# A gradient over rows: stores on a second DMA queue, issued in pairs with loads, the load held back by a pass of DVE

## The chip, the cores and the metric

The kernel runs on one core of one Trainium2 chip. The metric is the device time of one execution in microseconds (us), as a median over runs; lower is better. The profile is of one execution, and its own times count from the first instruction of the program. VectorE is called DVE, GpSimd POOL, ScalarE ACT and SyncE SP, as in the profile.

## The reference

```python
x = np.random.randn(8192, 8192).astype(np.float32)
np.gradient(x, axis=1)
```

For each of 8192 rows of 8192 float32 values: inside the row, element j of the result is half of x[j+1] - x[j-1]; at the two ends it is the one-sided difference, x[1] - x[0] and x[8191] - x[8190], not halved. 268.44 MB are read and 268.44 MB are written.

## The kernel before

The 8192 rows are cut into 32 sets (`nsets`) of 256 rows. A set is two neighbouring rows on each of 128 partitions (`R = 2`), so a partition holds 2 x 8192 = 16384 contiguous float32, 64 KB, and one transfer of a set is 8.39 MB. On chip there are three slots (`NB = 3`), each of 64 + 16384 columns. A load writes set i into columns 64 and up of slot i mod 3 (`SH = 64`); the result is built in the same slot from column 0 on, 64 columns to the left of what it is made from, and is stored from there.

For each set, in the order of the program:

- POOL (L70) computes the four unhalved end differences of each partition (two rows, two ends) into the small tile `ends`. It waits for the load of the set.
- DVE (L76) makes one custom pass over 16382 columns: element j+2 minus element j, times 0.5. It waits for POOL. At the four places that are row ends it writes values of no use.
- DVE or, for twelve of the sets, POOL (L87) copies the four values from `ends` over those places.
- SP (L89) issues the store of the set.

Everything that moves data is issued by SP, so there is one DMA queue, in the order in which SP issues. Three loads are issued at the start. After every third set, three more loads follow, and load i waits for the store of set i - 3, which used the same slot. The queue so carries three stores, then three loads, and so on; the last group has two of each.

`manual_schedule` keeps the order as written. The helper `chain` takes the place of the automatic dependencies: an instruction waits for those that are named as `needed`, and for the one in front of it on its engine where that one belongs to the same slot.

Of the kernel before, what the change touches and what calls it, by code (L numbers as in the profile page):

```python
# [1 line left out]

# [4 lines left out]


@with_exitstack
def kernel(  # L10
    ctx: ExitStack,
    tc: tile.TileContext,
    x: bass.AP,
    out: bass.AP,
):

    nc = tc.nc
    P = nc.NUM_PARTITIONS
    n, m = x.shape
    R = 2
    NB = 3  # L30
    SH = 64
    W = R * m
    nsets = n // (P * R)
    f32 = x.dtype

    x_sets = x.rearrange("(s p t) m -> s p (t m)", p=P, t=R)
    out_sets = out.rearrange("(s p t) m -> s p (t m)", p=P, t=R)

    pool = ctx.enter_context(tc.tile_pool(name="pool", bufs=1))
    slots = [pool.tile([P, SH + W], f32, name=f"slot{k}", tag=f"slot{k}") for k in range(NB)]  # L40
    ends = pool.tile([P, nsets, R, 2], f32, name="ends", tag="ends")
    loads, stores = [], [None] * nsets
    in_front = {}

    def chain(i, ins, *needed):

        group, engine = f"slot{i % NB}", ins.ins.engine
        keep = [o.ins for o in needed]  # L50
        if in_front.get(engine, (None,))[0] == group:
            keep.append(in_front[engine][1])
        tc.declare_no_dep(ins.ins, group=group, keep=keep, reason="implied by the needed step")
        tc.add_to_no_dep_group(group, ins.ins)
        in_front[engine] = group, ins.ins
        return ins

    def load(i):
        b = slots[i % NB]
        ins = nc.sync.dma_start(out=b[:, SH : SH + W], in_=x_sets[i])  # L60
        loads.append(chain(i, ins, *([stores[i - NB]] if i >= NB else [])))

    with tc.manual_schedule():
        for i in range(NB):
            load(i)
        for i in range(nsets):
            b = slots[i % NB]
            xin = b[:, SH : SH + W].rearrange("p (t m) -> p t m", m=m)

            ins = nc.gpsimd.tensor_sub(  # L70
                out=ends[:, i, :, :],
                in0=xin[:, :, 1 : m : m - 2],
                in1=xin[:, :, 0 : m - 1 : m - 2],
            )
            at = [chain(i, ins, loads[i])]
            ins = nc.vector._custom_dve(  # L76
                dve_ops.TENSOR_TENSOR_REDUCE_SUB_MAX,
                out=b[:, 1 : W - 1],
                in0=b[:, SH + 2 : SH + W],
                in1=b[:, SH : SH + W - 2],  # L80
                s0=0.0,
                s1=0.5,
            )
            halved = chain(i, ins, *at)
            res = b[:, 0:W].rearrange("p (t m) -> p t m", m=m)
            placer = nc.gpsimd if i % 5 in (1, 3) and i < nsets - 2 else nc.vector
            ins = placer.tensor_copy(out=res[:, :, 0 : m : m - 1], in_=ends[:, i, :, :])  # L87
            placed = chain(i, ins, halved)
            ins = nc.sync.dma_start(out=out_sets[i], in_=b[:, 0:W])  # L89
            stores[i] = chain(i, ins, placed)  # L90
            if i % NB == NB - 1:
                for k in range(i + 1, min(i + 1 + NB, nsets)):
                    load(k)


# [1 line left out]
_INS = ['x']  # L97
_OUTS = [((8192, 8192), 'float32')]


# [23 lines left out]
```

## Time and profile before

| | |
|---|---|
| time, median of 3 runs | 1248.12 us (1246.43 to 1248.73) |
| span of the profiled execution | 1245.7 us; its own time is not listed beside it |
| DVE busy | 554.6 us (45%), 52 instructions |
| POOL busy | 8.8 us (1%), 48 instructions |
| DMA queue q1 | 9216 packets, 536.88 MB, 99.8% of 16 engines' span |
| DMA rate | 431 GB/s, mean over the span |
| L76, the pass over a set | 32 times, mean 17224 ns |
| L87, the copy of the ends | 20 times on DVE, mean 172 ns; 12 times on POOL, mean 190 ns |
| L70, the end differences | 32 times on POOL, mean 198 ns |
| issue to landing, median | loads 58.0 us, stores 40.4 us |

How to read it: busy times of an engine are the sum of its instructions' durations; issuing a DMA is not counted as busy. A DMA transfer is spread over 16 DMA engines, and each engine works through its own share of rows; a transfer has landed when all 16 have reported. "From issue to landing" therefore includes the time that a transfer stands in the queue behind others. In the timeline a row has the start, the duration, the engine, the line, the operation, and in brackets how long the engine had been idle and what ended that. A row of a table of windows has the window and its length, busy time and number of instructions of DVE and POOL, the clock, and then the DMA engines' share and rate; a packet is counted in the window in which it begins, so in short windows the share can be over 1.

### The profile page before, as it was taken

What the parts mean: (1) busy time and instruction counts of PE and PEld (TensorE: products, weight loads), DVE (VectorE), ACT (ScalarE), POOL (GpSimd) and SP (SyncE); (2) the same over time, 40 slices, a digit from 0 to 9 for tenths busy, and PEclk for the clock granted to TensorE, in tenths of its full rate; (3) what the DMA queues carried; (4) which work ended last, traced back from release to release, by engine and by line L of the source; (5) the groups of instructions that cost most, each with busy time, mean ns of one, the idle gap of its engine ahead of it and who ended that gap; (6) DMA issues with size and microseconds to landing.
All of it is one profiled execution on the core that took longest, in us unless ns stands there. A gap on an engine that the chain in (4) does not pass through costs nothing.

```text
span 1245.7 us, 237 instructions
## 1 busy us (share of the span) xinstructions
DVE 554.6 (45%) x52; POOL 8.8 (1%) x48
## 2 busy tenths in 40 slices
DVE  2850583069009702850582079009603840591083
POOL 0000000000000000000000000000000000000000
DMA  9999999999999999999999999999999999999999
GB/s 404 438 436 423 427 431 438 438 438 436 436 427 431 425 438 436 425 434 436 429 434 436 434 436 434 436 434 438 419 436 436 434 438 438 431 434 429 429 410 404
DMA packets 9217, 536.88 MB, mean 431 GB/s; under 512 B 1024, under 2 KB 1024, under 8 KB 1024
## 3 DMA queue, kind: packets, MB, share of 16 engines
q1 hardware_dynamic: 9216, 536.88, 99.8%
q14 instruction: 1, 0.01, 0.0%
HBM read 268.44 MB, written 268.44 MB: 431 GB/s over the span
## 4 chain that ended last, share of the span: by engine, by line
another core or an unknown queue 74%; DVE 18%; DMA 3%; issue 2%; POOL 1%; SPq 0%; POOLq 0%
DVE slot L76 18%; DMA slot<-in_x_dram 3%; POOL ends L70 0%; POOL slot L87 0%; SPq L60 0%; POOLq L119 0%; DVE slot L87 0%
## 5 line engine op out<-in xcount | busy, mean ns | idle before, releaser
L76 DVE CUSTOM_DVE_ANT_0 slot<-slot 128x16382 f32<-128x16382 f32 x32 | 551.2, 17224 | 668.7 <-POOL ends L70 668.7
L70 POOL TENSOR_TENSOR ends<-slot 128x4 f32<-128x4 f32 x32 | 6.3, 198 | 989.6 <-DMA slot<-in_x_dram 989.6
L87 POOL COPY slot<-ends 128x4 f32<-128x4 f32 x12 | 2.3, 190 | 207.9 <-DVE slot L76 207.9
L87 DVE COPY slot<-ends 128x4 f32<-128x4 f32 x20 | 3.4, 172 | 0.7
L108 POOL MEMSET const-bfloat16-1.0<- 128x1 bf16 x1 | 0.1, 101 | 0.0
L108 POOL MEMSET const-uint8-127<- 128x1 uint8 x1 | 0.1, 101 | 0.0
L108 POOL MEMSET const-float32-0.0<- 128x1 f32 x1 | 0.1, 98 | 0.2 <-issue 0.2
L108 POOL MEMSET const-float32-1.0<- 128x1 f32 x1 | 0.1, 98 | 0.0
## 6 DMA issues: line engine op xcount, KB each, us to landing
slot<-in_x_dram SPq DMA_DIRECT2D x32, 58.0
out_dram<-slot SPq DMA_DIRECT2D x32, 40.4
```

Source lines behind the costliest of these rows:

```text
L70: ins = nc.gpsimd.tensor_sub(out=ends[:, i, :, :], in0=xin[:, :, 1 : m : m - 2], in1=xin[:, :, 0 : m - 1 : m - 2],)
L76: ins = nc.vector._custom_dve(dve_ops.TENSOR_TENSOR_REDUCE_SUB_MAX, out=b[:, 1 : W - 1], in0=b[:, SH + 2 : SH + W], in1=b[:, SH : SH + W - 2],
L87: ins = placer.tensor_copy(out=res[:, :, 0 : m : m - 1], in_=ends[:, i, :, :])
L108: nc = _bacc.Bacc("TRN2", target_bir_lowering=False, num_devices=1)
```

## The change

Stores are issued by ACT, loads by SP, each in a queue of its own. Two loads are issued at the start instead of three. From then on load i + 2 (`ahead`) belongs to store i.

Before the copy of the ends of set i, DVE makes a pass of 8 columns (`FIRST`) that waits for the landing of store i - 1 (for i from 1 to 30); the copy, and with it store i, come after it on DVE. After the copy, DVE makes a pass of 1700 columns (`THEN`), and load i + 2 waits for that pass. Both passes read a tile of zeros, `still`, which POOL sets once, and write into the slot that load i + 2 will overwrite, the one that store i - 1 has left. They are the same custom operation as the pass over a set, and their results are not used. All copies of the ends are made by DVE.

```diff
-    def load(i):
+    def load(i, *needed):
         b = slots[i % NB]
         ins = nc.sync.dma_start(out=b[:, SH : SH + W], in_=x_sets[i])
-        loads.append(chain(i, ins, *([stores[i - NB]] if i >= NB else [])))
+        loads.append(chain(i, ins, *needed))
+
+    def difference(out, x, width):
+        return nc.vector._custom_dve(
+            dve_ops.TENSOR_TENSOR_REDUCE_SUB_MAX,
+            out=out,
+            in0=x[:, 2 : 2 + width],
+            in1=x[:, 0:width],
+            s0=0.0,
+            s1=0.5,
+        )
+
+    def pause(i, at, width, *needed):
+        ins = difference(slots[i % NB][:, at : at + width], still, width)
+        return chain(i, ins, *needed)
 
     with tc.manual_schedule():
-        for i in range(NB):
+        for i in range(NB - 1):
             load(i)
...
             halved = chain(i, ins, *at)
             res = b[:, 0:W].rearrange("p (t m) -> p t m", m=m)
-            placer = nc.gpsimd if i % 5 in (1, 3) and i < nsets - 2 else nc.vector
-            ins = placer.tensor_copy(out=res[:, :, 0 : m : m - 1], in_=ends[:, i, :, :])
+            ahead = i + NB - 1
+            if 0 < i < nsets - 1:
+                pause(ahead, SH, FIRST, stores[i - 1])
+            ins = nc.vector.tensor_copy(out=res[:, :, 0 : m : m - 1], in_=ends[:, i, :, :])
             placed = chain(i, ins, halved)
-            ins = nc.sync.dma_start(out=out_sets[i], in_=b[:, 0:W])
+            ins = nc.scalar.dma_start(out=out_sets[i], in_=b[:, 0:W])
             stores[i] = chain(i, ins, placed)
-            if i % NB == NB - 1:
-                for k in range(i + 1, min(i + 1 + NB, nsets)):
-                    load(k)
+            if ahead < nsets:
+                load(ahead, pause(ahead, SH + FIRST, THEN))
```

`FIRST, THEN = 8, 1700` stands with the other constants, and `still` is `pool.tile([P, 2 + THEN], f32)`, set by `nc.gpsimd.memset(still, 0.0)` ahead of the loops.

More of the change, by code (lines that the diff above doesn't have):

```diff
@@ L31 @@
     SH = 64
+    FIRST, THEN = 8, 1700
     W = R * m
@@ L41 @@
     ends = pool.tile([P, nsets, R, 2], f32, name="ends", tag="ends")
+    still = pool.tile([P, 2 + THEN], f32, name="still", tag="still")
+    nc.gpsimd.memset(still, 0.0)
     loads, stores = [], [None] * nsets
@@ L75 @@
             at = [chain(i, ins, loads[i])]
[L76 to L83, printed above, removed]
+            ins = difference(b[:, 1 : W - 1], b[:, SH : SH + W], W - 2)
             halved = chain(i, ins, *at)
             res = b[:, 0:W].rearrange("p (t m) -> p t m", m=m)
-            placer = nc.gpsimd if i % 5 in (1, 3) and i < nsets - 2 else nc.vector
-            ins = placer.tensor_copy(out=res[:, :, 0 : m : m - 1], in_=ends[:, i, :, :])
+            ahead = i + NB - 1
+            if 0 < i < nsets - 1:
+                pause(ahead, SH, FIRST, stores[i - 1])
+            ins = nc.vector.tensor_copy(out=res[:, :, 0 : m : m - 1], in_=ends[:, i, :, :])
             placed = chain(i, ins, halved)
-            ins = nc.sync.dma_start(out=out_sets[i], in_=b[:, 0:W])
+            ins = nc.scalar.dma_start(out=out_sets[i], in_=b[:, 0:W])
             stores[i] = chain(i, ins, placed)
-            if i % NB == NB - 1:
-                for k in range(i + 1, min(i + 1 + NB, nsets)):
-                    load(k)
+            if ahead < nsets:
+                load(ahead, pause(ahead, SH + FIRST, THEN))
 _INS = ['x']
```

## The prediction

> **What bounds the kernel now.** I read the page first: engines, DMA rows, queues.
>
> ```profile
> DVE 554.6 (45%) x52; POOL 8.8 (1%) x48
> DMA  9999999999999999999999999999999999999999
> GB/s 404 438 436 423 427 431 438 438 438 436 436 427 431 425 438 436 425 434 436 429 434 436 434 436 434 436 434 438 419 436 436 434 438 438 431 434 429 429 410 404
> DMA packets 9217, 536.88 MB, mean 431 GB/s; under 512 B 1024, under 2 KB 1024, under 8 KB 1024
> q1 hardware_dynamic: 9216, 536.88, 99.8%
> ```
>
> The 16 DMA engines are the bound: one queue, busy 99.8% of a span of 1245.7 us, while VectorE (DVE) works 45% of it. 9216 packets are 64 transfers x 16 engines x 9: eight rows of 64 KB and one 4-byte completion. The change moves the same bytes, so it can win only what the queue loses to slow packets, and it can lose whatever makes an engine wait or slows a packet.
>
> To see what is lost I took the timeline. A `POOL L70` starts about 0.07 us after a load has landed, so its start times are the landings:
>
> ```profile
> 22.71 0.20 POOL L70 TENSOR_TENSOR ends<-slot 128x4 f32<-128x4 f32 x1 [22.27 <-DMA slot<-in_x_dram]
> 42.04 0.20 POOL L70 TENSOR_TENSOR ends<-slot 128x4 f32<-128x4 f32 x1 [19.13 <-DMA slot<-in_x_dram]
> ...
> 62.44 0.20 POOL L70 TENSOR_TENSOR ends<-slot 128x4 f32<-128x4 f32 x1 [2.69 <-DMA slot<-in_x_dram]
> ...
> 954.88 0.20 POOL L70 TENSOR_TENSOR ends<-slot 128x4 f32<-128x4 f32 x1 [59.57 <-DMA slot<-in_x_dram]
> ...
> 974.22 0.20 POOL L70 TENSOR_TENSOR ends<-slot 128x4 f32<-128x4 f32 x1 [19.15 <-DMA slot<-in_x_dram]
> ...
> 993.55 0.20 POOL L70 TENSOR_TENSOR ends<-slot 128x4 f32<-128x4 f32 x1 [19.13 <-DMA slot<-in_x_dram]
> ```
>
> Load 1 lands 19.33 us after load 0, load 2 another 20.40 us later; in the late group both steps are 19.33 to 19.34. A load followed by a load takes 19.33 to 19.36 everywhere. The third load of a group, which has a store behind it in the queue, takes 20.40, 19.45, 19.51, 20.05, 19.85, 19.79, 19.45, 19.84, 19.33, 19.36 in the ten groups: mean 19.70, so a change from load to store costs 0.36 us on average, 0 to 1.06, and 3.6 us in all. A change from store to load shows nothing over 0.05. The windows show the same in packets (a row counts the packets that begin in it):
>
> ```profile
> 57.90:60.37 2.47, 1.60 (x1) 0.19 (x1) 1.00 1.42 425
> 60.37:61.42 1.05, 0.00 (x0) 0.00 (x0) 1.00 0.00 0
> 61.42:62.10 0.68, 0.00 (x0) 0.00 (x0) 1.00 3.57 1542
> 1204.62:1205.39 0.77, 0.00 (x0) 0.00 (x0) 1.00 0.00 0
> 1205.46:1205.60 0.14, 0.00 (x0) 0.00 (x0) 1.00 16.42 7022
> ```
>
> The first three: load 2's last packets begin at about 58 and should end 2.42 us later, but no packet begins for another 1.05 us. The last two price a store's start from nothing: store 30 is issued at 1204.62 while 15 engines are idle, no data begins before 1205.39, and the 15 first packets come at 1205.47 to 1205.59, 0.85 to 0.97 us after issue (each 2.45 us instead of 2.42).
>
> **The change, part by part.** Each queue now has one direction. Per iteration DVE waits for store i-1, does an 8-column pass, copies the two end columns, store i leaves from ScalarE's (ACT) queue, DVE passes 1700 columns, load i+2 leaves from SP. So store i and load i+2 share the engines; I call that a pair, and there are 30 (stores 0 to 29 with loads 2 to 31).
>
> Seam, from the landing of store i-1 to the first packet of store i: last packet to semaphore 0.40 us (store 30: last data at 1225.16, last update at 1225.56); semaphore to DVE about 0.07 (as POOL above); the pass of 8 columns about 0.17 (17.22 us for 16382 columns is 1.04 ns a column and some 0.16 fixed); 0.03; the copy 0.17 (L87, mean 172 ns); 0.03 to the issue; 0.85 to 0.97 to data. Sum 1.72 to 1.84 us. ACT issues no DMA in this trace; I price its start like SP's row, bound it by zero and by the coldest row (the first load: issue 0.74, first packets 1.75 to 2.43, so up to 1.7), and take 0.91 because it is the warm one. With 1.7 the seam is 2.55.
>
> Its cover is the tail of load i+1. The pass of 1700 columns takes 1700 x 1.04 ns + 0.16 = 1.93 us, so the load comes about 1.98 us behind its store, inside the store's first packet (2.42). If the engines take packets from the two queues in turn, they do store, load, store, load, and each ends with one load packet of 2.41 us after the last store packet. 2.41 covers 1.72 to 1.84 with about 0.6 to spare; an engine that is ahead of the slowest by more than that idles, but only to be level with it. Nothing is lost at the seam then. If that cover were gone, it is 1.8 us x 30 = 54.
>
> DVE's waiting instruction has the copy, the 1700 pass and the difference of set i+1 behind it. After store i-1 lands at T, the pass ends at about T+2.4, which is when load i+1 lands; the difference ends at T+20, and the next store lands at T+38.7. Per pair DVE has 17.22 + 0.17 + 0.17 + 1.93 = 19.5 us of work: 18 us of slack. The twelve copies that go from POOL (190 ns) to DVE (172) and the memset of 1702 columns (POOL idles 22.27 us first) are under this cover: nothing. SP no longer holds stores between loads; its new wait is for the 1700 pass only, with only later loads behind.
>
> The beginning stays: loads 0 and 1, then store 0, ready at 40.40 and at the engines at 41.3, when load 1's data is ending (landed 41.98). The end stays covered too: store 30 leaves when store 29 has landed, beside load 31's tail; store 31 is ready 17.22 + 0.17 + 0.2 after load 31 lands, inside store 30's 19.34.
>
> The sum: landing of load 0 at 22.71, then 63 transfers x 19.34 = 1218.4, then 0.83 from the last landing to the span's end as now (1244.84 to 1245.67), less the 0.07 counted twice: 1241.9 us against 1245.7. That is 3.8 less: the ten direction changes (3.6) and a little at store 30. The runs' median, 1248.12, stands 2.4 above the profiled span (the lowest run 0.8 above, the profiled run's own time is not given beyond its span), so 1248.1 - 3.8 = 1244.3.
>
> What this leaves open is the price of alternating. No row has two queues at work. The nearest is the direction change within one queue, 0 to 1.06 us. With 8 changes from load to store in each of 30 pairs, 240 in all, zero is lost at the low end and 87 us at the mean price (254 at the highest). I take zero for the forecast: the delay sits in the last load packet of a queue whose next transfer goes the other way, all engines show it even when they reach that point 3 us apart, and in the changed kernel no queue ever turns. That is an inference and not a row, hence the odds below. Below zero there is nothing much: 2.42 us per 64 KB is what every undisturbed packet takes, in either direction.
>
> One rule speaks against taking turns row by row. The Trainium skill, "DMA: Bandwidth & Descriptors", section "Queues, rings and completion order", says that an engine goes round its queues a whole packet at a time, a packet being typically 9 to 17 descriptors; no run here shows which unit that is on these queues. The Trainium skill, same page, section "Anatomy of one DMA" puts a transfer's fixed cost at about 2.0 us where the store's rows here give 0.4 + 0.9; by it the estimated seam would be 2.5 us, not 1.8, and the cover of 2.41 just used up.
>
> **The rivals.**
>
> 1. *Whole transfers alternate.* If an engine drains all nine entries of the store before it looks at the load, the order is store, load, store, load by transfers, the seam has 19 us of cover, but the engine turns once per pair: 30 x 0.36 = 10.9 on 1244.3 gives 1255, slower. For it: the nine entries belong to one transfer. Against: nothing in the trace. It turns the gain into a loss once a turn costs over 3.8 / 30 = 0.13 us. (The packet of 9 to 17 descriptors in the Trainium skill, "DMA: Bandwidth & Descriptors", section "Queues, rings and completion order", would do this here.)
>
> 2. *Every change from load to store costs, across queues too.* 240 x 0.36 = 87 gives 1331; at 0.02, which the two best groups do not exceed, 4.8 gives 1249. Break-even with before is 3.8 / 240 = 16 ns a change, and eight of the ten groups show over 0.1 us. For it: the only row on mixed directions. Against: the two late groups, and the argument above. I see it spread between 1249 and 1331.
>
> 3. *The seam is not covered.* If the load does not outlast the store, because the two share unevenly or the load's first packet comes first on some engines (then the store ends last), each pair idles: 0.3 us x 30 = 9 gives 1253, 1.8 x 30 gives 1298. For it: a margin of only 0.6 us, and engines up to 3 us apart late in the trace. Against: the shared wait brings them level in each pair, and the slowest engine never idles while the 0.6 holds.
>
> 4. *It does nothing that can be measured*: part of the 3.8 is given back. A difference under 0.2% (2.5 us; the three runs spread over 0.18%) cannot be told from none.
>
> **How the numbers follow.** Forecast mechanism 0.46, its own range 1242 to 1248: 0.38 of it is faster by over 0.2% (under 1245.6), 0.08 within. Rival 1: 0.16. Rival 2: 0.22. Rival 3: 0.10. Rival 4: 0.04 within, and 0.02 for an end earlier than I can account for. Faster 0.40, same 0.12, slower 0.48: the likeliest single case is the gain, but the slower cases together outweigh it. The range runs from 1241 to 1300: it takes in rivals 1 and 3 and the lower half of 2, and leaves out the upper part of 2 (0.12) and the earliest ends (0.03).
>
> **What would show it.** Right: the landings of consecutive loads 38.6 to 38.7 us apart from load 2 to load 31; a store's landing about 2.4 us before its partner load's; issue of the next store about 0.9 us after that landing; DMA share of the two queues near 100% in sum; slow load packets gone. Rival 1: store to landing about 20 us instead of 37, landings of loads 19 us after the stores'. Rival 2: a pair over 39 us with no engine idle and packets above 2.42 us. Rival 3: the pair long, packets at 2.42 us, and windows without packet starts after each store's landing. If DVE's difference ends later than the store it should precede, the slack of 18 us was wrong.

## The result, and the profile after

The changed kernel takes 1300.22 us (median, 1297.22 to 1302.07) against 1248.07 us: ratio 1.0416, 95% interval 1.0401 to 1.0431. It is 4.2% slower; forecast were 1244.3 us and a range up to 1300.0.

The page after, the lines that answer to those of before:

```profile
DVE 613.8 (47%) x124; POOL 8.1 (1%) x37
DMA  9999999999999999999999999999999999999998
GB/s 419 387 419 419 419 419 419 419 419 419 419 415 391 419 418 419 387 389 419 450 389 411 395 419 419 419 415 403 407 419 419 419 419 413 425 405 401 419 419 387
DMA packets 9217, 536.88 MB, mean 413 GB/s; under 512 B 1024, under 2 KB 1024, under 8 KB 1024
q10 hardware_dynamic: 4608, 268.44, 49.7%
q1 hardware_dynamic: 4608, 268.44, 49.6%
```

The same 9216 packets and bytes, now half on each queue. The engines are "busy" for 49.7 + 49.6 = 99.3% of a span of 1300.3 us, hardly less than the 99.8% of before. So most of the lost time did not go into gaps but into longer packets: 0.993 x 1300.3 x 16 / 8192 = 2.52 us per 64 KB row, where before has 0.998 x 1245.7 x 16 / 8192 = 2.43.

Where the long rows are, the timeline says. One seam of the changed kernel:

```profile
241.53 0.17 DVE L56 CUSTOM_DVE_ANT_0 slot<-still 128x8 f32<-128x8 f32 x1 [19.70 <-DMA out_dram<-slot]
241.62 0.16 DVE L88 COPY slot<-ends 128x4 f32<-128x4 f32 x1
241.69 1.92 DVE L56 CUSTOM_DVE_ANT_0 slot<-still 128x1700 f32<-128x1700 f32 x1
241.81 0.34 ACTq L90 DMA_DIRECT2D out_dram<-slot  x1
243.64 0.33 SPq L52 DMA_DIRECT2D slot<-in_x_dram  x1
243.98 0.20 POOL L76 TENSOR_TENSOR ends<-slot 128x4 f32<-128x4 f32 x1 [39.40 <-DMA slot<-in_x_dram]
```

A store has landed just before 241.53; 0.28 us later the next store is issued (241.81), 1.83 us after that its load (243.64), and the old load lands 2.45 us after the old store (243.98). All of this is as forecast. The pair is not: from landing to landing of the loads (`POOL L76` starts) it takes 39.45 to 42.06 us, from 83.97 to 1260.17 on average 40.56, instead of 38.6 to 38.7. The windows of this seam and of another show what is late (a row is counted where it begins; 1 MB in a window is 16 rows, one per engine):

```profile
243.00:243.50 0.50, 0.50 (x1) 0.00 (x0) 1.00 6.64 2097
243.50:246.10 2.60, 2.00 (x2) 0.20 (x1) 1.00 0.00 0
246.10:247.00 0.90, 0.90 (x1) 0.00 (x0) 1.00 2.69 1165
488.25:488.35 0.10, 0.10 (x1) 0.00 (x0) 1.00 1.78 655
525.70:526.60 0.90, 0.00 (x0) 0.00 (x0) 1.00 0.01 0
526.70:528.08 1.38, 1.08 (x3) 0.00 (x0) 1.00 0.00 0
528.10:528.30 0.20, 0.20 (x1) 0.00 (x0) 1.00 11.56 4915
528.30:530.50 2.20, 1.61 (x2) 0.20 (x1) 1.00 0.09 30
532.90:533.20 0.30, 0.30 (x1) 0.00 (x0) 1.00 9.45 3277
533.20:535.70 2.50, 2.50 (x1) 0.00 (x0) 1.00 0.06 26
535.60:536.60 1.00, 1.00 (x1) 0.00 (x0) 1.00 3.61 983
```

*First seam.* The load's last rows end at 243.02 to 243.46 and the store's first rows begin directly behind them: no idle time at all. But the next rows begin at 246.16 to 246.99, so those first rows took 3.1 to 3.55 us, not 2.42. If a row's data takes 2.42 here as everywhere, then, counted back from the ends, it flowed from about 244.2 (243.7 to 244.6), which is 2.4 us after issue; the row's record would open early and contain the wait. The windows do not show this directly; the stores-only run, below, supports it.

*Second seam.* Here one engine is a row behind the other 15. It fell behind at the seam before, where its first store row began at 488.30 (the single row of that window) and the others' at 486.30 to 487.08. So now its store is complete one row later (526.6 against 523.7 to 524.2), and the landing waits for it. The other 15 engines ran dry at 526.1 to 526.6; the next store was issued at 527.27, and its first rows came at 528.12 to 528.27, 0.85 to 1.00 us after issue, at 2.45 to 2.48 us each. But then, when the load joins, the third store rows (from 533.0) take 2.65 to 3.5 us and the load's first rows 3.1 to 4.6 (window of 535.60: 15 rows).

The packet records are the trace's list of all rows with start and duration. They do not name the engine, so rows are chained where one begins as another ends. Over all pairs they give 1.66 us of excess row time (above 2.42 a row) and 0.22 us of idle time per engine and pair. They lie in two places. At the seam, 0.8 us are lost: 0.57 in the store's first rows and the idle time. Where the load joins, 1.1 us are lost: 0.29 in the store's later rows, mostly the third, and 0.80 in the load's, mostly the first. In the 11 pairs of 29 with under 0.03 us of idle time, the seam costs 0.76 to 0.90 us and the load's start 0.3 on average; in the other 18, where some or most engines ran dry, the load's start costs 1.6 on average. Everywhere else the rows alternate store, load, store, load at 2.42 us, without a loss.

### The profile page after: what moved, and what is told of

The parts are those of the page before. It is cut to its first block, busy times and chain, and to the rows that moved or that the text cites. A ratio compares the mean times of both kernels' runs of the same rounds, so it can differ in the third digit from the quotient of the medians.

```text
span 1300.3 us, 325 instructions
## 1 busy us (share of the span) xinstructions
DVE 613.8 (47%) x124; POOL 8.1 (1%) x37
## 3 DMA queue, kind: packets, MB, share of 16 engines
q10 hardware_dynamic: 4608, 268.44, 49.7%
q1 hardware_dynamic: 4608, 268.44, 49.6%
## 4 chain that ended last, share of the span: by engine, by line
DMA 92%; DVE 3%; issue 3%; POOL 0%; POOLq 0%
DMA out_dram<-slot 87%; DMA slot<-in_x_dram 5%; DVE slot L56 3%; DVE slot L88 0%; POOL ends L76 0%; POOLq L119 0%
## 5 line engine op out<-in xcount | busy, mean ns | idle before, releaser
L56 DVE CUSTOM_DVE_ANT_0 slot<-still 128x1700 f32<-128x1700 f32 (+1 forms) x60 | 62.3, 1045 | 618.3 <-DMA out_dram<-slot 618.3
L76 POOL TENSOR_TENSOR ends<-slot 128x4 f32<-128x4 f32 x32 | 6.4, 199 | 1251.7 <-DMA slot<-in_x_dram 1251.7
```

What stands on the lines that cost most here:

```text
L56: return nc.vector._custom_dve(dve_ops.TENSOR_TENSOR_REDUCE_SUB_MAX, out=out, in0=x[:, 2 : 2 + width], in1=x[:, 0:width], s0=0.0, s1=0.5,)
L76: ins = nc.gpsimd.tensor_sub(out=ends[:, i, :, :], in0=xin[:, :, 1 : m : m - 2], in1=xin[:, :, 0 : m - 1 : m - 2],)
```

## The experiments

Theories: **A (entry)**, rows are slow where a transfer joins engines at work; **B (alternation)**, taking turns between the directions costs; **C (seam)**, the engines run short of work between a store's landing and the next store's data, because the store has to wait for that landing.

**One queue.** Tells queues from pairing.

```diff
-            ins = nc.scalar.dma_start(out=out_sets[i], in_=b[:, 0:W])
+            ins = nc.sync.dma_start(out=out_sets[i], in_=b[:, 0:W])
```

> The changed kernel with its stores issued by SP, so that one queue carries store, load, store, load as whole transfers; all waits and both passes stay. Theory A (entry): in the changed kernel the 64 KB rows are slow only where a transfer joins engines that are at work on the other queue, at the head of each pair, about 1.7 us of slow rows a pair, and alternating afterwards is free. Then one queue takes this away and leaves 30 turns from load to store at the 0.36 us of before: about 1252 to 1256 us. Theory B (alternation): the slow rows come from two directions taking turns row by row; one queue ends that too: also 1252 to 1256. Theory C (the pairing itself, each store behind a landing, starves the engines): the waits are the same, so it stays near 1300.

Measured: 1250.41 us, ratio 1.0023 (1.0013 to 1.0032). All three expectations missed, A and B by little. The waits and the passes cost next to nothing by themselves. C as written, with the waits alone as the cause, is wrong; it had overlooked that whole transfers alternate here, so that the seam lies under a load of 19 us. C stands only as a lack of cover. A and B both stand.

**No hold.** The second pass is shortened to 8 columns.

```diff
-    FIRST, THEN = 8, 1700
+    FIRST, THEN = 8, 8
```

> The changed kernel with the second pass cut from 1700 columns to 8, so the load is issued about 0.2 us behind its store instead of 2.0. Theory A: the load joins a row earlier, the entry still costs about 1.7 us a pair, and the tail that covers the seam shrinks, so idle time comes on top: 1300 to 1330. Theory B: the number of turns stays the same, 1300. Theory C: with the tail gone each pair idles up to 1.8 us more: up to 1350.

Measured: 1382.25 us, ratio 1.1081 (1.1064 to 1.1097), beyond all three. The pairs take 43.0 us. Store and load now land together:

```profile
480.59 0.17 DVE L56 CUSTOM_DVE_ANT_0 slot<-still 128x8 f32<-128x8 f32 x1 [25.21 <-DMA out_dram<-slot]
480.81 0.20 POOL L76 TENSOR_TENSOR ends<-slot 128x4 f32<-128x4 f32 x1 [42.69 <-DMA slot<-in_x_dram]
```

So nothing covers the seam. The packet records have about 2.2 us idle and 2.1 us of long rows in each pair, the latter in the first rows of the store (0.74) and of the load (1.34). B, which saw no change, falls; C had the direction right and the size too small.

**Long hold.** Five passes in place of one.

```diff
-                load(ahead, pause(ahead, SH + FIRST, THEN))
+                for k in range(5):
+                    held = pause(ahead, SH + FIRST + k * THEN, THEN)
+                load(ahead, held)
```

> The changed kernel with five passes of 1700 columns instead of one before each load, so the load is issued about 9.4 us behind its store. Both queues still share the engines for about half of each transfer, and the load's tail is some 9 us. Theory A: the idle time goes (about 7 us in all), and the slow rows stay wherever a transfer joins: 1275 to 1295. Theory B: half as many turns, half of the loss: about 1270. Theory C: the seam is covered five times over, all the loss goes: 1243 to 1248.

Measured: 1251.43 us, ratio 1.0031 (1.0019 to 1.0043). Its timeline and windows:

```profile
437.19 0.20 POOL L76 TENSOR_TENSOR ends<-slot 128x4 f32<-128x4 f32 x1 [40.90 <-DMA slot<-in_x_dram]
473.49 0.32 POOL L76 TENSOR_TENSOR ends<-slot 128x4 f32<-128x4 f32 x1 [36.10 <-DMA slot<-in_x_dram]
514.61 0.20 POOL L76 TENSOR_TENSOR ends<-slot 128x4 f32<-128x4 f32 x1 [40.81 <-DMA slot<-in_x_dram]
```

```profile
240.00:502.00 262.00, 180.00 (x51) 1.85 (x7) 1.00 1.00 433
502.00:764.00 262.00, 186.03 (x56) 1.76 (x7) 1.00 1.00 432
```

Two pairs take 36.30 + 41.12 = 77.4 us, 38.7 each: the rate of undisturbed rows, although 10 of the 16 rows of a pair follow a row of the other queue. The slow rows went with the idle time. So A falls too in its plain form: joining is free when the engines have enough left to do. C holds, in both signs of the edit. The 3 us above its range are at the end: load 31 lands late (1211.64), and the engines run dry behind store 30 while DVE works on set 31 (a DMA share of 0.27 from 1221 to 1230).

**The order of before, stores on ACT.** One edit to the kernel before.

```diff
-            ins = nc.sync.dma_start(out=out_sets[i], in_=b[:, 0:W])
+            ins = nc.scalar.dma_start(out=out_sets[i], in_=b[:, 0:W])
```

> The kernel before with one change: stores are issued by ACT. No pass holds anything back, stores go when they are ready, loads when the store of their slot has landed. Theory A: transfers join engines at work about as often as in the changed kernel, unless a queue always holds its next transfer: 1260 to 1300. Theory B: rows alternate whenever both queues hold work: 1280 to 1310. Theory C: no store waits for a landing here, so the time of before, 1245 to 1250.

Measured: 1252.95 us, ratio 1.0051 (1.002 to 1.0082), with single runs from 1249.67 to 1269.75. The profiled one has a span of 1260.2 us and loses its time in one place, the end:

```profile
1221.00:1239.20 18.20, 17.39 (x2) 0.17 (x1) 1.00 0.07 29
```

Load 31 and store 30 end together, and for the 17.4 us of DVE's last pass the engines are idle (share 0.07). The pairs before that take 38.6 to 40.0 us, but for the first two (44.2 and 41.9). Long rows add up to 4.0 us per engine in the whole run, against 4.2 in the kernel before. Two queues in two directions cost nothing while each store is issued ahead of need.

**One direction at a time.** In the first of these two kernels stores 0 to 30 become loads, in the second loads 2 to 31 become stores.

```diff
-            ins = nc.scalar.dma_start(out=out_sets[i], in_=b[:, 0:W])
+            if i < nsets - 1:
+                ins = nc.scalar.dma_start(out=b[:, 0:W], in_=x_sets[i])
+            else:
+                ins = nc.scalar.dma_start(out=out_sets[i], in_=b[:, 0:W])
```

```diff
-        ins = nc.sync.dma_start(out=b[:, SH : SH + W], in_=x_sets[i])
+        if i < NB - 1:
+            ins = nc.sync.dma_start(out=b[:, SH : SH + W], in_=x_sets[i])
+        else:
+            ins = nc.sync.dma_start(out=out_sets[i], in_=b[:, SH : SH + W])
...
```

The dots in the second one stand for a memset of the third slot and for the end differences, which are computed for sets 0 and 1 alone. Neither kernel writes the gradient.

> The changed kernel with stores 0 to 30 replaced by loads of the same size and timing on ACT's queue (set i is read again into the slot where its result stood; of the output only the last set is written). All waits and both passes stay, so the seams are as short of cover as in the changed kernel, but every row goes from HBM to SBUF. If the slow rows at the head of a pair need the two directions: they vanish, pairs of 38.7 to 39.5, 1243 to 1265 us. If they are the price of starting on drained engines to read from HBM: they stay on both queues, 1290 to 1340.

> The changed kernel with loads 2 to 31 replaced by stores of the same size and timing on SP's queue (what stands in the slot is written to the rows of that set, which store i + 2 later writes again; a memset fills the third slot first, the end differences are left out from set 2 on, and the passes wait for those stores instead). Every row of the pairs goes from SBUF to HBM. If the slow rows need the two directions, or come from starting to read HBM: none, 1243 to 1265 us. If any start of a queue on drained engines costs, whatever it carries: 1280 to 1320.

Measured, one run each: 1290.2 and 1276.65 us. Neither answer came out clean. Per engine and pair, loads only: 0.70 us of long rows and 0.8 idle; stores only: 0.3 and 0.8; the changed kernel: 1.66 and 0.22. With stores only the split moves from 0.85 + 0.0 in the first pairs to 0.15 + 0.95 in the late ones, at a sum of 0.7 to 1.2 and with the same waits: long first row and idle time look like the same shortage, booked differently.

The places of the loss do come out clean. With one direction nearly all of it is at the seam, 1.4 and 1.0 us; all the rows behind the first ones on ACT's queue lose 0.1 together, the first rows on SP's queue included. The 1.1 us that the changed kernel loses where the load joins need both directions.

**Two passes, three passes.** The loop of the long hold, shortened.

```diff
-                for k in range(5):
+                for k in range(2):      # and range(3)
```

> The changed kernel with two passes of 1700 columns instead of one: the load is issued about 3.8 us behind its store, so its tail past the store's completion is one or two rows longer. If the loss comes from seams that run out of cover (store arriving when the last load row or nothing is left), there is a threshold, and one more row of 2.4 us is enough: 1243 to 1252. If the loss falls with the time that the queues share, a line through 1300 at 2.0 us and 1251 at 9.4 us gives 1288.

> The changed kernel with three passes of 1700 columns: the load is issued 5.6 us behind its store. With two passes the pairs alternated, 36.7 and 44.1 us: a well covered seam makes the store wait for the load's tail while the hold runs from its issue, so the next tail is shorter. On average the tail is then (hold + seam) / 2: 2.7 us at one pass, 3.6 at two, 4.5 at three, 6.4 at five, against a seam of 3.4. Three passes should leave only now and then a short one: 1250 to 1265. If the loss goes with the shared time instead: 1276, on the line from 1300 to 1251.

Measured: 1296.99 us, ratio 1.0392 (1.0368 to 1.0415), and 1276.43 us, ratio 1.0228 (1.0212 to 1.0244). Both miss the value of C, and the second hits the 1276 of its rival, a loss that goes with the shared time. The landings with two passes:

```profile
447.20 1.57 POOL L76 TENSOR_TENSOR ends<-slot 128x4 f32<-128x4 f32 x1 [36.52 <-DMA slot<-in_x_dram]
491.27 0.20 POOL L76 TENSOR_TENSOR ends<-slot 128x4 f32<-128x4 f32 x1 [42.51 <-DMA slot<-in_x_dram]
527.87 1.56 POOL L76 TENSOR_TENSOR ends<-slot 128x4 f32<-128x4 f32 x1 [36.40 <-DMA slot<-in_x_dram]
571.90 0.20 POOL L76 TENSOR_TENSOR ends<-slot 128x4 f32<-128x4 f32 x1 [42.47 <-DMA slot<-in_x_dram]
```

Pairs of 44.1 and 36.6 us take turns, 40.3 on average against 38.7. The hold runs from the store's *issue*. After a well covered seam the store still waits for the load's tail while the hold runs, so its lead, and with it the next tail, is short; that seam runs dry, the store starts at once and leads by the full hold, and the next tail is long again. The averaged tail of (hold + seam) / 2 took this for a swing that dies out; it does not. The packet records show where it is paid: behind a covered seam the load's start loses 0.05 us, behind a dry one 2.0. With three passes the seams still alternate (43.4 and 36.2 us); only every second one pays, and the mean pair (39.54 us from 88.46 to 1235.14) is 0.90 over the floor of 38.64: 29 x 0.90 = 26 us over the long hold's level of 1251. The straight line by shared time gave 1276 too, but it missed at two passes by 9 us (1288), and the order of before with stores on ACT, where 12 of 16 rows follow one of the other queue, loses nothing in its pairs.

**Store not held.** The pass that waits for the landing moves behind the store's issue.

```diff
-            if 0 < i < nsets - 1:
-                pause(ahead, SH, FIRST, stores[i - 1])
             ins = nc.vector.tensor_copy(out=res[:, :, 0 : m : m - 1], in_=ends[:, i, :, :])
             placed = chain(i, ins, halved)
             ins = nc.scalar.dma_start(out=out_sets[i], in_=b[:, 0:W])
             stores[i] = chain(i, ins, placed)
+            if 0 < i < nsets - 1:
+                pause(ahead, SH, FIRST, stores[i - 1])
```

> The changed kernel with the pass of 8 columns moved behind the issue of the store: store i goes when its result is ready, and the landing of store i-1 holds back only load i+2 (with the 1700 pass, unchanged). Theory now: a transfer that joins busy engines needs about 2.5 us from issue to its first data (0.9 on idle ones), so the seam from store landing to store data is about 3.4 us and one row of 2.4 us does not cover it; the missing time shows as long rows as much as idle time. Here the store's queue is issued ahead, so the seam is covered whatever the load's hold: pairs of 38.6 to 39.2, 1245 to 1262 us (the upper end if the engines run dry behind the last load, as they do for 18 us with stores on ACT in the order of before). Rival: two queues with a load held 1.9 us behind something cost in themselves: 1290 to 1300.

Measured: 1252.24 us, ratio 1.0029 (1.0017 to 1.0042), with two of the six single runs at 1270.9. The profile is of one of these two:

```profile
80.00:1160.00 1080.00, 534.12 (x111) 5.59 (x28) 1.00 1.00 431
1230.00:1250.00 20.00, 17.40 (x2) 0.06 (x1) 1.00 0.16 69
```

Its pairs run at 431 GB/s, with 0.3 us of long rows a pair and no idle time; it loses its 17 us at the end, where the engines have nothing to do while DVE works on set 31. Same two queues, same 1700 columns in front of the load; what is gone is the store's wait for the landing, and with it 48 us. (The load, still held by the landing, now comes some 14 us behind the issue of its store.) This is the part of the change that costs.

**A longer seam.** The first pass is lengthened by 960 columns.

```diff
-    FIRST, THEN = 8, 1700
+    FIRST, THEN = 968, 1700
```

> The changed kernel with the first pass at 968 columns instead of 8, which puts 1.0 us into the seam and nothing else. If the seam is short of cover in every pair and each missing microsecond is paid: 30 x 1.0 more, 1325 to 1335. If the loss is slow rows that do not depend on the seam's length, and the seam itself is covered: 1298 to 1305.

Measured: 1322.48 us, ratio 1.0597 (1.0583 to 1.0611): 22 us more for 30 x 1.0 us, just under the value for a seam that is short in every pair; about three quarters of what is put into the seam is paid. Its packet records show the two kinds of start in alternate pairs: on idle engines a store's rows begin 0.84 to 0.90 us after issue, and the load's start then loses 2.0 us; on engines that still have a load row to do, data flows 2.8 to 3.2 us after issue (medians of the engines, first row's end less 2.42), and the load's start loses nothing.

**Two attempts at a faster version.** The long hold with two passes before load 31 alone, and the order of before with stores 0 to 26 on ACT and the rest on SP.

```diff
-                for k in range(5):
+                for k in range(5 if ahead < nsets - 1 else 2):
...
-            ins = nc.sync.dma_start(out=out_sets[i], in_=b[:, 0:W])
+            ins = (nc.scalar if i < 27 else nc.sync).dma_start(out=out_sets[i], in_=b[:, 0:W])
```

> Five passes before each load, as in the long-hold run (1251.4), but two before the last one, load 31. In the long-hold run load 31 landed so late that the engines ran dry while DVE worked on set 31; about 8 us by its timeline. If that is where its last microseconds went: 1243 to 1246, which is under the kernel before. If the long hold costs in every pair: 1250 to 1252.

> The order of before with stores 0 to 26 on ACT and 27 to 31 on SP. With all stores on ACT nothing was lost in the pairs (4.0 us of slow rows in all, as before), but the engines were idle for 17.8 us at the end, where the last load and the last but one store ended together. The end of before, one queue, has no such wait. If that was all: 1245 to 1249, level with before or just under it.

Measured: 1249.83 us, ratio 1.0016 (1.0007 to 1.0025), and 1253.74 us, ratio 1.0043 (1.0022 to 1.0065; single runs 1249.16 to 1275.19). Both miss their ranges (1243 to 1246 and 1245 to 1249). The first gives back part of the end, the second does not gain reliably, and why its runs spread so far is open. No version beat the kernel before.

## Why the prediction was wrong

**The bound, the start and DVE's cover: right.** DVE's 20 us behind the landing, the copies, the memset and SP's new wait are hidden, as 241.53 to 243.98 shows.

**Taking turns at no cost: right.** Rival 2 had a chance of 0.22; the long hold runs its pairs at 38.7 us with 10 turns in 16 rows. The Trainium skill, "DMA: Bandwidth & Descriptors", section "Queues, rings and completion order", has an engine drain a whole packet, typically 9 to 17 descriptors, before it switches to another queue. In the packet records of this case they switch after every 64 KB row, and the 4-byte completion takes a turn of its own, so whole transfers do not alternate and rival 1 is out.

**The step that failed is the seam.** In "Sum 1.72 to 1.84 us" the term "0.85 to 0.97 to data" was read from the one store that started on idle engines. In this kernel the store starts beside the load's last rows, and where engines hardly ran dry its data comes 2.1 to 2.7 us after issue. The bound that was set on that term, 1.7, was too low as well. The steps ahead of it were priced well: the store is issued 0.66 us (median) after the last completion entry of the one before, for a sum of 0.87. So the true seam is 2.8 to 3.3 us, and one row of 2.41 does not cover it. "Nothing is lost at the seam then" should have read "0.8 us". The seam of 2.5 us that the prediction estimates with the Trainium skill, "DMA: Bandwidth & Descriptors", section "Anatomy of one DMA", is under the measured one too; that section fits its fixed cost to transfers that GpSimd issues, and none here is.

**A second term was put at nothing: the load's start.** The prediction lets the load come "inside the store's first packet" and has no price for it. The runs show 1.1 us a pair there, more than at the seam itself. It is not the price of joining as such, which the long hold has at 0.03 us. It follows a seam that ran dry: 1.6 us on average in such pairs of the changed kernel, and 2.0 with 968 columns or with two passes, where covered seams have 0.1 at most.

**The cover was mis-sized too.** That "the shared wait brings them level in each pair" does not hold. An engine that has fallen a row behind stays behind through the pair, its completion entry comes last, and the other 15 wait for it and run dry (the second seam above). And the tail is not set by the hold alone, as the alternating pairs show.

**Rival 3 named the place; its price fits by luck.** The 1298 stood for 1.8 us of idle engines with no cover at all. Measured are only 0.2 us idle; 0.6 of long store rows and 1.1 at the load's start, for which the rival has no term, make up the rest. Its chance was 0.10 because of "a margin of only 0.6 us". The sign in the profile that was named for it, "packets at 2.42 us, and windows without packet starts", was mostly wrong, as most of the shortage is inside the first rows. The sum of the landings closes: 29 x (40.56 - 38.64) = 55.7 (38.64 being the mean pair of the long hold), the first pair 42.06 - 38.64 = 3.4, less the 3.6 of turns from load to store that the prediction meant to save: 55.5, against 1300.3 - 1245.7 = 54.6.

**What stays open:** why a load that joins a store just started from idle engines loses up to 2 us. The runs show the conditions, a dry seam and two directions, but not the mechanism; and that a long row is a row that waits is an inference from the stores-only run.

## What to carry to other kernels

A transfer that is made to wait for another's landing has a seam of landing, semaphore, instructions and start, and its start must be priced on engines in the state in which they will be: in this case 0.9 us on idle engines, 2.1 to 2.7 us on engines with one 64 KB row left to do. Price the transfer that joins next as well: behind a seam that ran dry it lost up to 2 us more. Keep the next transfer of at least one queue issued before the last one lands (as before does with one queue, or with the store left free), and do not read a DMA share of 99% as full use: compare the mean packet time with that of an undisturbed packet. Where a delay is counted from an issue, ask whether the transfer starts at its issue in every round; if not, rounds may alternate instead of settling.

## What the runs showed of the hardware

Loads and stores on two queues share the 16 engines row by row at the full rate: 433 GB/s over 262 us of the long hold, against 431 for the whole of before. A row's recorded duration seems to contain a wait for its data: first rows of 3.1 to 4.6 us beside 2.42, so that the engines show as 99.3% busy in a kernel that is 4% slower. And a store's completion waits its turn behind a whole row of the other queue: in the first seam the last store rows end at 238.19 to 238.63, and their completion entries come at 240.6 to 241.04, one row of 2.42 us later.
